# Rotary embedding on one core: tiles of 8 positions held in place from load to store, with the first and last tile in pieces and the tables on the load queue

## The chip, the cores and the metric

The kernel runs on one core of one Trainium2 chip. The metric is device time in microseconds (us), the median of several executions. All runs told of here were in the fast state, with a granted clock of 1.00 in every profile. A profile's span is some 1.5 to 2.3 us shorter than the median time.

## The reference

`x` is float32 of shape (8, 2048, 16, 64), 67.11 MB; `cos` and `sin` are (2048, 32), 262 KB each. Each pair of neighbouring elements of a head is rotated by the angle of its position:

```python
x1, x2 = x_pairs[..., 0], x_pairs[..., 1]
out1 = x1 * cos - x2 * sin
out2 = x1 * sin + x2 * cos
out = np.stack([out1, out2], axis=-1)      # float32, the shape of x
```

So 134.74 MB must pass between HBM, the chip's main memory, and the core, whatever the kernel does; the profile counts 134.76 MB, with 0.02 MB of instructions.

## The kernel before

A tile is 128 partitions with 4 positions each: 4096 float32 per partition, 16 KB, 2.1 MB in all. There are 32 tiles. For each, the sync engine's queue loads it; ScalarE (ACT) rounds it to bfloat16 ("halve"); VectorE (DVE) makes two products with tables and one sum ("rotate"); ACT widens the result into an output buffer and issues the store from its own queue.

```python
K = 4; NX = 5                       # positions per partition; x buffers
# pools: xt x 5 (16 KB), xh qt pt x 2 (8 KB each), ot x 4 (16 KB)

def load(i):    nc.sync.dma_start(out=xt, in_=x_t[b, g])
def halve(i):   nc.scalar.copy(out=xh, in_=xt)                  # to bf16
def rotate(i):  # qt = xh * sin_table ; pt = xh * cos_table ; pt += swap(qt)
    ...
def store(i):
    nc.scalar.copy(out=ot, in_=pt)                              # to f32
    nc.scalar.dma_start(out=out_t[b, g], in_=ot)

load(0)
nc.scalar.dma_start(out=cos_sb, in_=cos_t)      # both on ACT's queue
nc.scalar.dma_start(out=sin_sb, in_=sin_t)
for i in range(1, NX): load(i)
# ... DVE builds s_tab and c_tab from sin_sb and cos_sb ...
halve(0)
for i in range(n):
    if i + 1 < n: halve(i + 1)
    rotate(i); store(i)
    if i + NX < n: load(i + NX)
```

Order matters on ACT, which runs its list in order: a store that has to wait holds back every halving behind it. The library that places the waits has eight completion semaphores for DMAs and gives them out in turn, so each DMA must also wait until the one eight places before it has landed (read from the instruction list of the built kernel).

## Time and profile before

| | before |
|---|---|
| time, median | 329.98 us (329.9 to 330.17) |
| span of the profile | 328.5 us |
| DVE busy, ACT busy | 218.3 us (66%), 230.8 us (70%) |
| moved, mean rate | 134.76 MB, 410 GB/s |
| sine table landed | 34.6 us |
| first store issued | 46.4 us |

Three views matter. The slices give, for each fortieth of the span, the busy share of an engine in tenths and the rate of the DMAs. The busy time by stretches gives the same for stretches that one chooses. The waits say who waited for whom. The prediction below shows lines of each. The timeline, in order of start, shows what the wait does (start us, duration us, engine, line, operation, and in brackets the idle time before it with its releaser; ACTq and SPq are the queues from which ACT and the sync engine issue DMAs):

```profile
34.63 0.45 DVE L102 CAST s_tab<-sin_sb 128x512 bf16<-128x512 f32 x1 [34.63 <-DMA sin_sb<-in_sin_dram]
42.75 3.61 ACT L91 CAST ot<-pt 128x4096 f32<-128x4096 bf16 x1 [25.37 <-DVE pt L85]
46.39 0.37 ACTq L92 DMA_DIRECT2D out_dram<-ot  x1
```

The sine table's cast starts the moment the table has landed; ACT had stood 25.37 us with two tiles halved when it widened the first result; the first store follows. Until then the output direction of the DMAs had nothing to do.

### The profile page before, as it was taken

How to read it: one execution, taken by the hardware profiler on the slowest of the kernel's cores; microseconds unless marked ns; L12 is line 12 of the kernel's file. 1: busy time of each engine (PE TensorE's matmuls, PEld its weight loads, DVE VectorE, ACT ScalarE, POOL GpSimd, SP SyncE). 2: the span in 40 equal slices, each digit the busy share in tenths (PEclk: the TensorE clock that was granted, in tenths of full speed). 3: DMA queues.
4: the chain of work that ended last, by engine and by line, in shares of the span. 5: the costliest groups of instructions: out<-in, count | busy, mean ns of one | idle time of the engine just before them, and what ended most of it. 6: DMA issues, size and time to landing. Idle time of an engine off the chain costs nothing.

```text
span 328.5 us, 334 instructions
## 1 busy us (share of the span) xinstructions
DVE 218.3 (66%) x99; ACT 230.8 (70%) x65; POOL 0.2 (0%) x4
## 2 busy tenths in 40 slices
DVE  0000798899999999866668866667876666876910
ACT  1710079999999999676786676687677678669740
POOL 0000000000000000000000000000000000000000
DMA  7999739999999999999999999999999999999997
GB/s 295 427 423 425 268 140 353 405 427 435 427 435 429 437 425 437 424 435 427 436 427 435 427 435 429 433 429 433 429 433 429 433 429 433 429 435 427 435 427 315
DMA packets 10275, 134.76 MB, mean 410 GB/s; under 512 B 1057, under 2 KB 2081, under 8 KB 2081
## 3 DMA queue, kind: packets, MB, share of 16 engines
q1 hardware_dynamic: 4608, 67.11, 48.7%
q10 hardware_dynamic: 5664, 67.64, 48.4%
q14 instruction: 3, 0.02, 0.0%
HBM read 67.63 MB, written 67.11 MB: 410 GB/s over the span
## 4 chain that ended last, share of the span: by engine, by line
DMA 62%; ACT 24%; issue 5%; DVE 4%; ACTq 1%
DMA out_dram<-ot 52%; ACT ot L91 18%; DMA sin_sb<-in_sin_dram 10%; ACT xh L60 6%; DVE pt L85 1%; DVE qt L79 1%; DVE pt L80 1%; ACTq L92 1%; ACTq L96 0%; DVE s_tab L102 0%; DVE s_tab L103 0%; ACTq L91 0%; DVE c_tab L104 0%
## 5 line engine op out<-in xcount | busy, mean ns | idle before, releaser
L91 ACT CAST ot<-pt 128x4096 f32<-128x4096 bf16 x32 | 115.3, 3604 | 64.7 <-DMA out_dram<-ot 36.0
L60 ACT CAST xh<-xt 128x4096 bf16<-128x4096 f32 x32 | 115.4, 3605 | 19.5 <-ACT ot L91 12.4
L79 DVE TENSOR_TENSOR qt<-xh,s_tab 128x4096 bf16<-128x4096 bf16 x32 | 73.3, 2291 | 59.2 <-ACT xh L60 59.2
L85 DVE TENSOR_TENSOR pt<-pt,qt 128x4096 bf16<-128x4096 bf16 x32 | 73.3, 2292 | 1.1
L80 DVE TENSOR_TENSOR pt<-xh,c_tab 128x4096 bf16<-128x4096 bf16 x32 | 73.1, 2284 | 0.0
L102 DVE CAST s_tab<-sin_sb 128x512 bf16<-128x512 f32 x1 | 0.5, 454 | 34.6 <-DMA sin_sb<-in_sin_dram 34.6
L60 ACT ACT_TABLE_LOAD x1 | 1.3, 1283 | 1.8 <-issue 1.8
L104 DVE CAST c_tab<-cos_sb 128x1024 bf16<-128x1024 f32 x1 | 0.7, 684 | 0.0
L103 DVE TENSOR_SCALAR s_tab<-sin_sb 128x512 bf16<-128x512 f32 x1 | 0.4, 442 | 0.0
L130 POOL MEMSET const-bfloat16-1.0<- 128x1 bf16 x1 | 0.1, 102 | 0.0
L130 POOL MEMSET const-uint8-127<- 128x1 uint8 x1 | 0.1, 102 | 0.0
L130 POOL MEMSET const-float32-0.0<- 128x1 f32 x1 | 0.1, 99 | 0.2 <-issue 0.2
L130 POOL MEMSET const-float32-1.0<- 128x1 f32 x1 | 0.1, 99 | 0.0
## 6 DMA issues: line engine op xcount, KB each, us to landing
xt<-in_x_dram SPq DMA_DIRECT2D x32, 2048.0 KB, 31.0
out_dram<-ot ACTq DMA_DIRECT2D x32, 2048.0 KB, 32.0
cos_sb<-in_cos_dram ACTq DMA_DIRECT2D x1, 256.0 KB, 22.7
sin_sb<-in_sin_dram ACTq DMA_DIRECT2D x1, 256.0 KB, 33.4
```

Source lines behind the costliest of these rows:

```text
L60: nc.scalar.copy(out=xh, in_=loaded.pop(i))
L79: nc.vector.tensor_tensor(out=rows(qt), in0=rows(xh), in1=tab(s_tab), op=mult)
L80: nc.vector.tensor_tensor(out=rows(pt), in0=rows(xh), in1=tab(c_tab), op=mult)
L85: nc.vector.tensor_tensor(out=pt3, in0=pt3, in1=q_swap, op=add)
L91: nc.scalar.copy(out=ot, in_=rotated.pop(i))
L92: nc.scalar.dma_start(out=out_t[b, g], in_=ot)
L102: nc.vector.tensor_copy(out=s2[:, :, 0], in_=sin_flat)
L103: nc.vector.tensor_scalar_mul(s2[:, :, 1], sin_flat, -1.0)
L104: nc.vector.tensor_copy(out=c_tab.rearrange("p g k (i j) -> p (g k i) j", j=2), in_=cos_sb.rearrange("p g c -> p (g c)").to_broadcast([P, ...
L130: nc = _bacc.Bacc("TRN2", target_bir_lowering=False, num_devices=1)
```

## The change

The intent: larger packets and fewer DMAs (tiles of 8 positions, 32 KB per partition), no output buffers (the result goes back over x, so one buffer serves from load to store), a quick start (first tile in pieces, tables behind it on the load queue) and a short end (last tile in pieces). The buffers take 200 KiB per partition before and after. The diff is shortened: `...` marks what is left out, and the pool lines and the comments stand for longer code.

```diff
-    K = 4
+    K = 8
-    hpool: xh, qt, pt x 2;  opool: ot x 4
+    hpool: xh x 3, qt x 1;  no opool
+    first_runs = [(0, 1), (1, 2), (2, 4), (4, 8)]
+    last_runs  = [(0, 4), (4, 6), (6, 7), (7, 8)]
+    # load_runs / store_runs: whole tile, but first_runs for the load of
+    # tile 0 and last_runs for the load and the store of the last tile
+    # computing: two halves per tile; tiles 0 and n-1 by those runs
...
-        nc.vector.tensor_tensor(out=rows(pt), in0=rows(xh), in1=tab(c_tab), op=mult)
+        nc.vector.tensor_tensor(out=rows(xh), in0=rows(xh), in1=tab(c_tab), op=mult)
...
-        ot = opool.tile([P, W], fp32, name="ot")
-        nc.scalar.copy(out=ot, in_=rotated.pop(i))
-        nc.scalar.dma_start(out=out_t[b, g], in_=ot)
+        nc.scalar.copy(out=tiles[i][:, k0:k1], in_=rotated.pop(j)[:, : k1 - k0])
+        for r0, r1 in store_runs(i):
+            if r1 == k1:
+                nc.scalar.dma_start(out=out_t[b, g, :, r0:r1], in_=tiles[i][:, r0:r1])
+        if k1 == K and i + NX < n:
+            load(i + NX)
...
-        nc.scalar.dma_start(out=cos_sb, in_=cos_t)
-        nc.scalar.dma_start(out=sin_sb, in_=sin_t)
+        nc.sync.dma_start(out=cos_sb, in_=cos_t)
+        nc.sync.dma_start(out=sin_sb, in_=sin_t)
```

More of the change, by code (lines that the diff above doesn't have):

```diff
@@ L26 @@
     P = 128
-    K = 4
+    K = 8
     G = S // (P * K)
     D2 = D // 2
-    W = K * H * D
+    HD = H * D
     NX = 5
-    x_t = x.rearrange("b (g p k) h d -> b g p (k h d)", p=P, k=K)
-    out_t = out.rearrange("b (g p k) h d -> b g p (k h d)", p=P, k=K)
+    x_t = x.rearrange("b (g p k) h d -> b g p k (h d)", p=P, k=K)
+    out_t = out.rearrange("b (g p k) h d -> b g p k (h d)", p=P, k=K)
     cos_t = cos.rearrange("(g p k) c -> p g (k c)", p=P, k=K)
@@ L39 @@
     xpool = ctx.enter_context(tc.tile_pool(name="xpool", bufs=NX))
-    hpool = ctx.enter_context(tc.tile_pool(name="hpool", bufs=2))
-    opool = ctx.enter_context(tc.tile_pool(name="opool", bufs=4))
+    hpool = ctx.enter_context(tc.tile_pool(name="hpool", bufs=1))
     cos_sb = consts.tile([P, G, K * D2], fp32)
@@ L49, with load_runs, store_runs, halve @@
     n = len(groups)
-    loaded, halved, rotated = {}, {}, {}
+    first_runs = [(0, 1), (1, 2), (2, 4), (4, 8)]
+    last_runs = [(0, 4), (4, 6), (6, 7), (7, 8)]
+    def load_runs(i):
+        return first_runs if i == 0 else last_runs if i == n - 1 else [(0, K)]
+    def store_runs(i):
+        return last_runs if i == n - 1 else [(0, K)]
+    pieces = []
+    for i in range(n):
+        runs = first_runs if i == 0 else last_runs if i == n - 1 else [(0, 4), (4, 8)]
+        pieces += [(i, k0, k1) for k0, k1 in runs]
+    tiles, halved, rotated = {}, {}, {}
     def load(i):
         g, b = groups[i]
-        xt = xpool.tile([P, W], fp32, name="xt")
-        nc.sync.dma_start(out=xt, in_=x_t[b, g])
-        loaded[i] = xt
-    def halve(i):
-        xh = hpool.tile([P, W], bf16, name="xh")
-        nc.scalar.copy(out=xh, in_=loaded.pop(i))
-        halved[i] = xh
-    def rotate(i):
+        tiles[i] = xpool.tile([P, K, HD], fp32, name="xt")
+        for k0, k1 in load_runs(i):
+            nc.sync.dma_start(out=tiles[i][:, k0:k1], in_=x_t[b, g, :, k0:k1])
+    def halve(j):
+        i, k0, k1 = pieces[j]
+        halved[j] = hpool.tile([P, 4, HD], bf16, name="xh", bufs=3)
+        nc.scalar.copy(out=halved[j][:, : k1 - k0], in_=tiles[i][:, k0:k1])
+    def rotate(j):
+        i, k0, k1 = pieces[j]
         g, _ = groups[i]
-        xh = halved.pop(i)
-        qt = hpool.tile([P, W], bf16, name="qt")
-        pt = hpool.tile([P, W], bf16, name="pt")
+        nk = k1 - k0
+        xh = halved.pop(j)
+        qt = hpool.tile([P, 4, HD], bf16, name="qt")
         def rows(a):
-            return a.rearrange("p (k h e) -> p k h e", k=K, h=H, e=D)
+            return a[:, :nk].rearrange("p k (h e) -> p k h e", h=H, e=D)
         def tab(a):
@@ L74, in tab, with widen @@
                 a,
-                offset=a.offset + g * K * D,
-                ap=[a.ap[0], [D, K], [0, H], [1, D]],
+                offset=a.offset + (g * K + k0) * D,
+                ap=[a.ap[0], [D, nk], [0, H], [1, D]],
             )
         nc.vector.tensor_tensor(out=rows(qt), in0=rows(xh), in1=tab(s_tab), op=mult)
-        nc.vector.tensor_tensor(out=rows(pt), in0=rows(xh), in1=tab(c_tab), op=mult)
+        nc.vector.tensor_tensor(out=rows(xh), in0=rows(xh), in1=tab(c_tab), op=mult)
         q_swap = dataclasses.replace(
-            qt, offset=qt.offset + 1, ap=[qt.ap[0], [2, W // 2], [-1, 2]]
+            qt, offset=qt.offset + 1, ap=[qt.ap[0], [2, nk * HD // 2], [-1, 2]]
         )
-        pt3 = pt.rearrange("p (a j) -> p a j", j=2)
-        nc.vector.tensor_tensor(out=pt3, in0=pt3, in1=q_swap, op=add)
-        rotated[i] = pt
-    def store(i):
-        g, b = groups[i]
-        ot = opool.tile([P, W], fp32, name="ot")
-        nc.scalar.copy(out=ot, in_=rotated.pop(i))
-        nc.scalar.dma_start(out=out_t[b, g], in_=ot)
+        xh3 = xh[:, :nk].rearrange("p k (a j) -> p (k a) j", j=2)
+        nc.vector.tensor_tensor(out=xh3, in0=xh3, in1=q_swap, op=add)
+        rotated[j] = xh
+    def widen(j):
+        i, k0, k1 = pieces[j]
+        nc.scalar.copy(out=tiles[i][:, k0:k1], in_=rotated.pop(j)[:, : k1 - k0])
+        g, b = groups[i]
+        for r0, r1 in store_runs(i):
[3 more added lines that the diff above has]
+            load(i + NX)
     with tc.manual_schedule():
         load(0)
-        nc.scalar.dma_start(out=cos_sb, in_=cos_t)
-        nc.scalar.dma_start(out=sin_sb, in_=sin_t)
+        nc.sync.dma_start(out=cos_sb, in_=cos_t)
+        nc.sync.dma_start(out=sin_sb, in_=sin_t)
         for i in range(1, NX):
@@ L108 @@
         halve(0)
-        for i in range(n):
-            if i + 1 < n:
-                halve(i + 1)
-            rotate(i)
-            store(i)
-            if i + NX < n:
-                load(i + NX)
+        for j in range(len(pieces)):
+            if j + 1 < len(pieces):
+                halve(j + 1)
+            rotate(j)
+            widen(j)
 _INS = ['x', 'cos', 'sin']
```

## The prediction

> **What bounds the kernel now.** I began with the page: is any compute engine full, and if not, what is? VectorE (DVE) is busy 66% of the span and ScalarE (ACT) 70%; the DMA row is at 9 in nearly every slice, except in three places. The first fence is the slice view: one character per fortieth of the span (8.2 us), then the rate moved in each slice.
>
> ```profile
> DVE  0000798899999999866668866667876666876910
> ACT  1710079999999999676786676687677678669740
> ...
> DMA  7999739999999999999999999999999999999997
> GB/s 295 427 423 425 268 140 353 405 427 435 427 435 429 437 425 437 424 435 427 436 427 435 427 435 429 433 429 433 429 433 429 433 429 433 429 435 427 435 427 315
> ```
>
> The reader is to see that the rate is 424 to 437 from the ninth slice to the last but one, and that the holes are slice 1, slices 5 to 8 and slice 40. To size the holes I asked for the busy time by stretches, cut where the rate changes (columns: stretch, length, DVE, ACT, POOL busy, clock, DMA share, GB/s):
>
> ```profile
> 0.00:4.00 4.00, 0.00 (x0) 1.28 (x1) 0.20 (x4) 1.00 0.57 165
> 4.00:32.00 28.00, 0.00 (x0) 7.21 (x2) 0.00 (x0) 1.00 1.01 422
> 32.00:48.00 16.00, 13.30 (x9) 4.81 (x2) 0.00 (x0) 1.00 0.53 202
> 48.00:62.00 14.00, 12.25 (x6) 13.15 (x5) 0.00 (x0) 1.00 0.98 366
> 62.00:324.00 262.00, 192.74 (x86) 204.38 (x57) 0.00 (x0) 1.00 1.01 431
> 324.00:328.50 4.50, 0.00 (x0) 0.00 (x0) 0.00 (x0) 1.00 0.49 211
> ```
>
> For 262 of 328.5 us the kernel moves 431 GB/s with the DMA engines full. The page gives 134.76 MB in all; at 431 GB/s that is 312.7 us. The rest of the span is lost DMA time, and each stretch's loss is its length times (1 - rate/431): 2.5 us at the start, 0.6 us from 4 to 32, **8.5 us** from 32 to 48, **2.1 us** from 48 to 62, 2.3 us at the end: 16.0, and 312.7 + 16.0 = 328.7, the span. So the ledger closes, and only the holes can be won.
>
> Why the middle hole? The waits, first of the engines, then of the loads' queue (SPq), say it:
>
> ```profile
> DVE s_tab L102 <- DMA sin_sb<-in_sin_dram: 34.6, 1, 34.6
> ACT ot L91 <- DVE pt L85: 28.7, 2, 25.4
> ...
> SPq L55 <- DMA cos_sb<-in_cos_dram: 20.1, 1, 20.1
> SPq L55 <- DMA sin_sb<-in_sin_dram: 10.8, 1, 10.8
> ```
>
> No rotation can start before the sine table is there, at 34.6 us, although it is 256 KB. ACT has halved two tiles by then and stands, the first store goes out at 46.4 us (timeline), and the five x buffers are not freed. The load queue itself waits for both tables: the instruction list of the kernel before shows eight completion semaphores taken in turn by all DMAs, so each DMA waits for the one eight places earlier; loads 5 and 6 come eight after the two tables. From 42 to 46 us the rate is 0.
>
> **What the Trainium skill says.** (1) "DMA: Bandwidth & Descriptors", section "Queues, rings and completion order": each DMA engine takes turns between queues that have work, a packet at a time. The trace agrees: the tables are 1,024 packets of 512 B on ACT's queue, 64 on each of 16 engines. At 431/16 = 26.9 GB/s a 16 KB packet of x takes 0.61 us; if each table packet waits for one of x, 64 take 39 us, 32 (cosine) 19.5. They landed 33.4 and 22.7 us after issue, and x had nothing to send for part of that time. (2) Same page, "Where 436 GB/s comes from": the fabric's ceiling is 435.2 GB/s. The trace sustains 431, so larger packets can win at most 1%, 3 us; I expect nearly none. (3) "SBUF — State Buffer", "SBUF size: 192, 224, or 256?": about 208 KiB per partition are usable. The sums below stay at 200; the trace cannot show it. (4) "VectorE: DVE Perf Modes", the section on the TRN2 errata: ScalarE needs 224 cycles plus one per element at 1.2 GHz. For 4096 elements 3.60 us; the trace has 3.605.
>
> **The change, part by part.** *Tables* move to the load queue, behind x's first tile, in front of the second. They no longer alternate with x packets. First tile plus tables are 4.19 + 0.52 = 4.72 MB; at 422 GB/s from 2.5 us on they end at 13.7; with an estimated 1 us to landing, 15 us. Against 34.6 that is **20 us earlier**, in compute. Table preparation costs 1.3 us as before (34.63 to 35.91 in the timeline).
>
> *First store.* Tile 0 is cut 1+1+2+4 of 8 positions. From the durations of 4096 elements (ACT 3.605, DVE 2.29), pieces of 1024 and 2048 cost by the formula of (4) 1.04 and 1.89 us on ACT; for DVE I estimate 0.69 and 1.22 (1.07 us saved per halving, as two bf16 per cycle at 0.96 GHz give). ACT works in order, halving one piece ahead: three operations per piece put the rotations at 16.3-18.4, 18.4-20.5, 21.3-25.0 and 25.9-32.8; ACT then halves the first half of tile 1, until 31.4, and widens from 32.8 to 36.4. The first store goes out at about **37 us** instead of 46.4, of 4.19 MB. Meanwhile five tiles are loading: 20.97 + 0.52 MB need 51 us at 422 GB/s, to 53 us. So stores join 16 us before the first loads are used up, and the engines **never run dry**. The losses of 8.5 and 2.1 us go away.
>
> *In-place result.* The output buffers go, and a tile is held from load to store: 5 x 32 KB, three xh and one qt of 8 KB, tables 8 KB, 200 KiB; before it was 5 x 16 + 4 x 16 + 6 x 8 + 8 = 200. The price is that a load waits for the landing of a store. In steady state a tile's load and store need 8.39 MB / 431 = 19.5 us, its compute the larger of ACT 4 x 3.605 + issues (15.1, twice the 7.52 between successive stores where the trace runs ACT-bound, 61.48 to 69.01) and DVE 6 x 2.29 = 13.7. Compute has 4.4 us of slack per tile. It holds up to two tiles, because a tile's last widening stands behind the halving of the next tile. Three remain with the DMAs; one would do to keep them full. Eight semaphores make each DMA wait for the one about four tiles back: loose enough.
>
> *Tail.* By my count the last load lands near 281 us; ACT gets through its last pieces near 298, while stores of three tiles remain, to 315. So the DMAs stay the bound to the end, then the last store needs its landing: the 2.3 us of before.
>
> *Compute totals.* ACT: 14 tiles x 14.42 + 2 x 15.15 = 232 us (before 231); DVE: 14 x 13.74 + 2 x 14.67 + 1.6 = 223 (before 218). All beside the DMAs.
>
> *Sum.* 312.7 + start 2.5 + about 0.6 for the loads-only rate + 0.3 for 1 and 4 KB packets (my estimate) + end 2.3 = 318.4 us of span. The medians lie 1.5 us above the span (329.98 against 328.5): **319.7 us**, 3.2% faster.
>
> **The rivals.** *Too few buffers.* Load waits for store, a round trip of 2 x 19.5 us plus compute; if compute held four of five tiles, the DMAs would thin out in mid-span. For it: the same 200 KiB are now freed in lumps of 32 KB. Against it: compute's slack. If it cost 0.5 us per tile, 16 tiles would make it 328. *Tracking by whole tile.* If the widening of the last tile's second piece waited for the store of its first (same buffer, other region), the final four pieces would go one by one behind landings, some 3 to 5 us each: about 328. The trace has no such case, so I cannot exclude it; I give it 7%. *The hidden gain.* Were the early hole only covering a later compute limit, nothing would come. Against it: from 62 to 324 us ACT works 204 of 262 us. *Faster packets.* At the ceiling of 435 the sum falls by 2.9 us, to 317.
>
> **Range and chances.** Most uncertainty is downward in gain: 316.5 to 324. Faster by over 2% needs less than 323.5 us: 0.86. Within 2%: 0.12, the rivals. Slower by over 2%: 0.02.
>
> **What would show it.** The sine table lands near 15 us and DVE starts near 16; the first store is issued near 37; the slices show no hole between the second and the last; the middle runs at 430 to 433; waits of the loads for stores are long on their queue but the DMA share stays at 1.0; at the end ACT is done some 15 us before the span. It is wrong if mid-span slices fall below 425, if the last stores stand apart from each other, or if a hole remains between 30 and 60 us.

## The result, and the profile after

The changed kernel takes **318.62 us** (318.48 to 319.15, 4 runs) against 330.0 of the kernel before on the same chip: a ratio of 0.9658, 95% interval 0.9641 to 0.9674. A ratio is the mean time of one kernel's fast runs over that of the other's of the same rounds, so not quite the ratio of the medians. The forecast was 319.7 us in a range of 316.5 to 324.0, so it held.

The slices of the kernel after:

```profile
DVE  0189999999999596693967939588440999999112
ACT  4078899999998692976949679495803999997322
...
DMA  7999999999999999999999999999999999999997
GB/s 304 424 463 405 455 397 401 459 438 422 455 405 463 397 460 401 459 414 448 443 418 455 405 459 405 455 405 459 418 443 447 414 428 430 424 433 439 442 414 302
```

The holes of slices 5 to 8 are gone: the DMA row is at 9 from the second slice to the last but one. By stretches:

```profile
0.00:4.00 4.00, 0.00 (x0) 1.28 (x1) 0.20 (x4) 1.00 0.53 168
4.00:32.00 28.00, 15.76 (x15) 14.69 (x8) 0.00 (x0) 1.00 1.03 437
32.00:48.00 16.00, 14.93 (x8) 15.20 (x5) 0.00 (x0) 1.00 0.98 406
48.00:62.00 14.00, 13.06 (x7) 13.54 (x5) 0.00 (x0) 1.00 1.04 449
62.00:312.00 250.00, 179.45 (x84) 184.89 (x56) 0.00 (x0) 1.00 1.00 432
312.00:316.90 4.90, 0.00 (x0) 0.40 (x1) 0.00 (x0) 1.00 0.57 232
```

The rate in single slices swings between 397 and 463, while the kernel before, with packets of 16 KB, had 424 to 437. I put that down to packets being booked as a whole (the DMA share of a stretch can pass 1.00, as the 1.04 above), so sums over longer stretches are what to read. Against the 431 GB/s of the ledger in the prediction the losses are 2.4 us at the start, 0 from 4 to 62 us (437, 406 and 449 offset each other), a gain of 0.6 from 62 to 312, and 2.3 at the end: 312.7 + 4.1 = 316.8, the span of 316.9. The waits of the engines, then of the load queue:

```profile
ACT xh L75 <- DMA xt<-in_x_dram: 61.6, 13, 12.7
DVE s_tab L121 <- DMA sin_sb<-in_sin_dram: 14.4, 1, 14.4
SPq L70 <- DMA out_dram<-xt: 241.9, 11, 51.4
```

The sine table is there at 14.4 us in place of 34.6. The load queue now stands 241.9 us for stores, as it must when a buffer is free only after its store, and the engines of the DMAs never run out of work over it: the longest total wait of the trace costs nothing. The two ends of the timeline, first store and last tile:

```profile
35.94 0.37 ACTq L109 DMA_DIRECT2D out_dram<-xt  x1
...
288.08 1.90 ACT L75 CAST xh<-xt 128x2048 bf16<-128x2048 f32 x1 [1.92 <-DMA xt<-in_x_dram]
299.00 1.04 ACT L75 CAST xh<-xt 128x1024 bf16<-128x1024 f32 x1 [5.52 <-DMA xt<-in_x_dram]
308.10 1.04 ACT L75 CAST xh<-xt 128x1024 bf16<-128x1024 f32 x1 [6.25 <-DMA xt<-in_x_dram]
312.43 0.34 ACTq L109 DMA_DIRECT2D out_dram<-xt  x1
```

The first store goes out at 35.9 us (46.4 before). The last tile's second, third and fourth piece land at 288.1, 299.0 and 308.1 us, and ACT, which waits for each (1.9, 5.5 and 6.3 us), issues the last store at 312.4, only 4.5 us before the end. That is not what the prediction had.

### The profile page after: what moved, and what is told of

The parts are those of the page before. It is cut to its first block, busy times and chain, and to the rows that moved or that the text cites. A ratio compares the mean times of both kernels' runs of the same rounds, so it can differ in the third digit from the quotient of the medians.

```text
span 316.9 us, 352 instructions
## 1 busy us (share of the span) xinstructions
DVE 223.2 (70%) x111; ACT 230.0 (73%) x73; POOL 0.2 (0%) x4
## 4 chain that ended last, share of the span: by engine, by line
DMA 62%; ACT 26%; DVE 4%; issue 3%; another core or an unknown queue 2%; SPq 1%; ACTq 1%
DMA xt<-in_x_dram 31%; DMA out_dram<-xt 28%; ACT xt L105 14%; ACT xh L75 12%; DMA sin_sb<-in_sin_dram 4%; DVE xh L100 1%; DVE xh L95 1%; DVE qt L94 1%; SPq L70 1%; ACTq L109 1%; DVE s_tab L121 0%; SPq L115 0%; DVE s_tab L122 0%; ACTq L105 0%
## 5 line engine op out<-in xcount | busy, mean ns | idle before, releaser
L75 ACT CAST xh<-xt 128x4096 bf16<-128x4096 f32 (+2 forms) x36 | 116.1, 3224 | 66.9 <-DMA xt<-in_x_dram 61.6
L105 ACT CAST xt<-xh 128x4096 f32<-128x4096 bf16 (+2 forms) x36 | 116.0, 3223 | 14.8 <-DVE xh L100 14.4
L94 DVE TENSOR_TENSOR qt<-xh,s_tab 128x4096 bf16<-128x4096 bf16 (+2 forms) x36 | 74.0, 2055 | 71.2 <-ACT xh L75 70.3
L100 DVE TENSOR_TENSOR xh<-xh,qt 128x4096 bf16<-128x4096 bf16 (+2 forms) x36 | 74.0, 2055 | 1.2
L95 DVE TENSOR_TENSOR xh<-xh,c_tab 128x4096 bf16<-128x4096 bf16 (+2 forms) x36 | 74.0, 2055 | 1.2
L121 DVE CAST s_tab<-sin_sb 128x512 bf16<-128x512 f32 x1 | 0.5, 453 | 14.4 <-DMA sin_sb<-in_sin_dram 14.4
## 6 DMA issues: line engine op xcount, KB each, us to landing
out_dram<-xt ACTq DMA_DIRECT2D x1, 2048.0 KB, 17.6
```

The lines of the kernel that those rows point to most:

```text
L75: nc.scalar.copy(out=halved[j][:, : k1 - k0], in_=tiles[i][:, k0:k1])
L94: nc.vector.tensor_tensor(out=rows(qt), in0=rows(xh), in1=tab(s_tab), op=mult)
L95: nc.vector.tensor_tensor(out=rows(xh), in0=rows(xh), in1=tab(c_tab), op=mult)
L100: nc.vector.tensor_tensor(out=xh3, in0=xh3, in1=q_swap, op=add)
L105: nc.scalar.copy(out=tiles[i][:, k0:k1], in_=rotated.pop(j)[:, : k1 - k0])
L121: nc.vector.tensor_copy(out=s2[:, :, 0], in_=sin_flat)
```

## The experiments

Eleven further kernels and the changed one again were run, all correct. "Before" was between 330.16 and 330.27 us on those chips.

| run | one edit | median us | ratio to before (95%) |
|---|---|---|---|
| e1 | before, tables behind the first load | 319.58 | 0.9676 (0.9661 to 0.9690) |
| e2 | before, tables behind the fifth load | 325.72 | 0.9860 (0.9846 to 0.9875) |
| e3 | after, tables on ACT's queue | 319.07 | 0.9659 (0.9643 to 0.9675) |
| e4 | e3, first tile not in pieces | 331.55 | 1.0035 (1.0022 to 1.0048) |
| e5 | after, last load whole | 318.61 | 0.9650 (0.9636 to 0.9663) |
| e6 | after, last store whole | 324.44 | 0.9825 (0.9811 to 0.9838) |
| e7 | after, last tile wholly as the others | 318.45 | 0.9644 (0.9631 to 0.9657) |
| e8 | after, three tiles held in place of five | 366.35 | 1.1113 (1.1082 to 1.1145) |
| e9 | after, tiles of 4, ten held | 329.95 | 0.9993 (0.9985 to 1.0001) |
| e10 | e9, last load whole | 321.46 | 0.9734 (0.9721 to 0.9748) |
| e11 | e10, eight held | 320.03 | 0.9692 (0.9679 to 0.9705) |
| after again | beside e9 | 318.73 | 0.9652 (0.9638 to 0.9665) |

### Which part of the change earns it?

**e1.** The kernel before with two words changed:

```diff
-        nc.scalar.dma_start(out=cos_sb, in_=cos_t)
-        nc.scalar.dma_start(out=sin_sb, in_=sin_t)
+        nc.sync.dma_start(out=cos_sb, in_=cos_t)
+        nc.sync.dma_start(out=sin_sb, in_=sin_t)
```

> The kernel before with one edit: both table loads go to the load queue behind the first x tile; tiles of 4, five x and four output buffers as before. Theory (the gain is the early hole, and the hole is the wait for the tables): sine lands near 10 us, the first store goes out near 22 us, no hole between 32 and 62 us, time 319 to 321 us, nearly all of the 11.4 us gained. Rival (large tiles, 32 KB packets or the in-place buffers earn it): the hole shrinks but the time stays above 325 us.

Measured: 319.58 us. The rate by slices of e1:

```profile
GB/s 273 416 429 431 429 431 429 433 433 433 437 433 431 429 429 429 428 431 431 430 429 433 431 439 431 433 433 429 429 429 429 431 431 429 431 433 433 437 431 316
```

From the waits of e1, the one for the sine table:

```profile
DVE s_tab L102 <- DMA sin_sb<-in_sin_dram: 10.4, 1, 10.4
```

The table is there at 10.4 us, the first store goes out at 22.8, and no hole is left. Of the 3.42% that the whole change saves, this edit alone saves 3.24%. The rival, that large tiles and in-place buffers earn the bulk of it, is out; the 0.18% left over for them is not clear of noise, as the intervals of e1 and of the kernel after overlap.

**e2.** The same two loads, but placed behind the fifth load of x.

> The kernel before with both table loads on the load queue, but behind all five first x loads. A middle dose. Theory: the tables land near 29 us (11.0 MB at 422 GB/s from 2.5 us on, and a little), so the first store goes out near 41 us, 5 us earlier than before and some 19 us later than with the tables behind the first tile; the seven loads that can run before the first store end near 38.5 us, so a hole of some 4.5 us and a slow start remain: 324 to 327 us. Rival (only the mixing of small packets with x packets cost time): as fast as with the tables behind the first tile, 319 to 321.

Measured: 325.72 us, inside the range. The table landed at 29.8 us, the first store went out at 41.56, and the slices show the shortened hole:

```profile
GB/s 294 426 444 393 324 304 361 434 432 430 436 428 432 434 430 432 429 432 428 433 436 428 430 436 428 432 432 432 430 430 438 430 430 436 426 432 430 434 430 324
```

Slices 4 to 7 hold 393, 324, 304 and 361 where before it was 425, 268, 140 and 353. Here the tables do not share turns with anything on another queue, and they still cost 6 us: it is the time at which they land that counts, through the first store, not the mixing as such.

**e3.** The kernel after with the tables back on ACT's queue (the diff of e1 reversed).

> The kernel after with the tables back on ACT's queue. Theory (taking turns packet by packet): 32 table packets per DMA engine now alternate with the 32 small packets of the first tile's four pieces, so the tables land with that tile, near 13 to 15 us, and the time stays within 0.5% of the kernel after, 318 to 320 us. Rival (the other queue as such delays them): they land past 25 us and the time goes past 322.

Measured: 319.07 us, ratio 0.9659 against 0.9658 of the kernel after. The table landed at 12.9 us. So in the changed kernel the queue of the tables does not matter, because the small packets of the first tile's pieces leave them their turns.

**e4.** e3, and the first tile loaded and computed as the others:

```diff
-        return first_runs if i == 0 else last_runs if i == n - 1 else [(0, K)]
+        return last_runs if i == n - 1 else [(0, K)]
-        runs = first_runs if i == 0 else last_runs if i == n - 1 else [(0, 4), (4, 8)]
+        runs = last_runs if i == n - 1 else [(0, 4), (4, 8)]
```

> The kernel after with the tables back on ACT's queue and the first tile loaded and computed as the others (one load of 32 KB packets, two halves). Theory: each of 32 table packets per engine waits for a 32 KB packet of 1.22 us, so sine lands near 40 us, the first store goes out near 60 us, five loads are used up at 53 us and load 5 waits for the first store: holes of 9 to 14 us, time 327 to 335 us, all of the gain lost. Rival (pieces of the first tile and the place of the tables do not matter): 319 us.

Measured: 331.55 us, 0.35% above the kernel before, so all of the gain is lost. The rate by slices of e4:

```profile
GB/s 326 428 426 449 406 445 127 191 381 354 409 445 445 433 433 405 445 441 434 441 417 429 438 441 441 413 425 441 441 441 433 413 433 445 437 433 431 429 405 288
```

From its timeline, the first widening, with ACT's idle time before it, and the first store:

```profile
50.81 3.60 ACT L105 CAST xt<-xh 128x4096 f32<-128x4096 bf16 x1 [30.25 <-DVE xh L100]
...
61.49 0.36 ACTq L109 DMA_DIRECT2D out_dram<-xt  x1
```

Sine lands at 42.5 us (estimated 40), the first store goes out at 61.5 (60), and slices 7 and 8 fall to 127 and 191 GB/s. The two tables have 32 packets per engine; if each waits for a 32 KB packet of x, 1.22 us at 26.9 GB/s, that makes 39 us. This is the 39 us that the prediction has for the kernel before, where 64 packets wait 0.61 us each: with tiles of 8 a wait is twice as long, but the tables have half as many packets, of 1 KB. e3 shows that the pieces of the first tile are a cure. The place in the queue is shown to be one for tiles of 4 (e1); for tiles of 8 without pieces it was not run by itself.

The five points together, in order of the sine table's landing:

| | sine landed | first store | time |
|---|---|---|---|
| e1 | 10.4 | 22.8 | 319.58 |
| after | 14.4 | 35.9 | 318.62 |
| e2 | 29.8 | 41.6 | 325.72 |
| before | 34.6 | 46.4 | 329.98 |
| e4 | 42.5 | 61.5 | 331.55 |

A first store before the first loads are used up costs nothing, however early it is (e1 against after). Beyond that each microsecond of delay costs about one (e2 to before: 4.8 us later and, on the same chip, 4.5 us longer). With tiles of 8 that point lies later, near 53 us by the prediction's count of 20.97 + 0.52 MB at 422 GB/s; with tiles of 4 only seven loads fit before the first store, 15.2 MB or 38.5 us. Counted from these two estimated points, e2, before and e4 are 3.1, 7.9 and 8.5 us late and lost 6.1, 10.7 and 12.5 us (against e1, e1 and e3): some 3 to 4 us are lost on top, whatever the delay. In the kernel before, the slow restart from 48 to 62 us is 2.1 of them; the rest was not traced.

### The last tile

**e5, e6, e7.** Why did the last load land at 308 us, not at 281? My theory was that the two queues take turns packet by packet, so a load of small packets beside stores of 32 KB packets gets a small share. The edits, in the two functions that cut the last tile:

```diff
 def load_runs(i):
-    return first_runs if i == 0 else last_runs if i == n - 1 else [(0, K)]
+    return first_runs if i == 0 else [(0, K)]            # e5, e7
 def store_runs(i):
-    return last_runs if i == n - 1 else [(0, K)]
+    return [(0, K)]                                      # e6, e7
 # e7 computes the last tile in two halves too
```

> The kernel after, with the last tile loaded whole (32 KB packets) while its computing and its stores stay in four pieces. Theory (queues take turns packet by packet, so a load of 16, 8 and 4 KB packets gets 1/3, 1/5 and 1/9 of the engines beside stores of 32 KB packets): the last load lands near 280 us instead of 308, ACT ends near 298 instead of 312; the time stays within 0.5% of the kernel after (317.5 to 319.5), because the bytes left are the same and the DMAs stay full. Rival (the last load came late because few loads were in flight): it lands past 300 us again.

> The kernel after, with the last tile stored in one piece, its load still in four. Theory: the last small piece of the load lands near 308 us, the store of 4.19 MB can go out only near 312 us, when the other stores are done, and needs 9.7 us alone plus its landing: 325 to 328 us, some 7 us lost. Rival (a backlog of stores covers it, as the prediction had it with ACT done at 298): 318 to 320 us.

> The kernel after, with the last tile treated as any other: loaded whole, computed in two halves, stored whole. Theory: the load lands near 280 us, its store goes out near 300 us while earlier stores still run, so the time stays within 0.6% of the kernel after (317.5 to 320.5): the pieces of the last tile only pay for the delay that they cause. Rival (stores in pieces at the end are needed as such): 324 us or more.

Measured: e5 318.61 us, e6 324.44 (0.6 below its range, but far from its rival's 318 to 320), e7 318.45. In the timeline of e5 the halving of the last tile starts when its load has landed, and the last store follows:

```profile
280.70 3.60 ACT L75 CAST xh<-xt 128x4096 bf16<-128x4096 f32 x1 [4.73 <-DMA xt<-in_x_dram]
...
302.92 0.34 ACTq L109 DMA_DIRECT2D out_dram<-xt  x1
```

The whole load of 4.19 MB lands at 280.7 us; cut in pieces to be early, its last piece landed at 308.1. So the rival of e5, too few loads in flight, is out. ACT's last store went out at 302.9, where 298 was expected. The size fits the theory: a piece of 0.524 MB in 4 KB packets beside 32 KB packets gets 4 of 36 bytes, and 0.524 x 9 / 431 GB/s is 10.9 us; the third piece took 299.0 - 288.1 = 10.9, the fourth 9.1. In e6 the late pieces meet a store that cannot go out before them; it was issued at 310.84 us. The rate by slices of e6:

```profile
GB/s 309 435 426 455 390 435 410 455 439 406 455 439 406 452 439 406 455 439 407 451 439 410 451 439 410 451 439 410 451 439 410 451 424 422 428 434 440 329 195 325
```

Slices 38 and 39 fall to 329 and 195 GB/s. With the load whole, e7 stores whole as well and loses nothing, because its store goes out at 302.6 us behind stores that still run. So the pieces of the last load cost 27 us of lead, and the pieces of the last store only pay for that. The net is zero: after, e5 and e7 have ratios of 0.9658, 0.9650 and 0.9644 whose intervals overlap. e7 is the best of the study by its median, but not clearly ahead of the changed kernel (which gave 0.9652 when run again); it is the simpler one.

### How many tiles must be held

**e8.** `NX = 5` becomes `NX = 3`.

> The kernel after with three tiles in place of five. The prediction had three of five with the DMAs where one would do. Theory: a tile of three is away for load and store at most 27 us of each 58 us cycle, less than the 2 x 19.5 us that a shared load and store take, so in turns only one queue has work and there are gaps behind each landing: 322 to 345 us, with mid-span slices below 425 GB/s. Rival (one in flight is enough): 318 to 320 us.

Measured: 366.35 us, 15% above the kernel after and beyond the range I gave. Its slices:

```profile
DMA  8995989799897997989989899898998979979998
GB/s 324 424 453 237 457 291 403 309 396 446 288 403 302 388 454 237 417 331 404 403 284 410 342 374 428 291 403 345 378 428 288 446 302 403 432 230 433 434 429 345
```

The rate swings between full and 230 to 300. ACT waits 107.3 us for loads (61.6 with five). A store must wait until the next tile has landed, because ACT halves one piece of the next tile first; with three tiles, load and store of the others then run side by side for 19 us (both land 19 us after issue, by the median) and are through almost together. In one round the load lands at 111.9 us and ACT works 7 us on it, so the next store is issued at 119.0; the next load is issued at 115.6, when the running store has landed; and from 114 to 116 us the rate is 0. Over the run this comes to 48 us, some 3 per tile. One tile in flight on average is not the same as one at every moment. Four tiles were not tried.

### The size of the tile alone

**e9.** The kernel after with tiles of 4, ten held in place, so the same bytes:

```diff
-    K = 8
+    K = 4
-    NX = 5
+    NX = 10
-    first_runs = [(0, 1), (1, 2), (2, 4), (4, 8)]
-    last_runs = [(0, 4), (4, 6), (6, 7), (7, 8)]
+    first_runs = [(0, 1), (1, 2), (2, 4)]
+    last_runs = [(0, 2), (2, 3), (3, 4)]
```

with one piece per other tile.

> The kernel after with tiles of 4 positions (16 KB packets), ten of them held, first and last tile in three pieces: the same bytes held, half the tile. It measures tile size alone. Theory (packet size earns at most the step from 431 to about 433 GB/s in mid-span): 318.5 to 320.5 us, within 0.5% of the kernel after. Rival (32 KB packets are a gain of their own): over 321 us, mid-span at 431 GB/s or less. A third way: eight semaphores in turn hold back loads of small tiles and leave gaps.

> The changed kernel itself, on the same chip in the same rounds as the run with tiles of 4, to compare the two: 318.6 us as before, within 0.3%.

Measured: 329.95 us, against 318.73 for the changed kernel in the same rounds. All of the gain was gone, which I had not expected. By its letter the rival holds (over 321 us, mid-span at 431 GB/s or less), but not in its reason: the mid-span runs at 431 as in the kernel before and in e1, which kept the gain. The loss is at the end. The end of e9 by stretches:

```profile
240.00:262.00 22.00, 4.88 (x3) 1.48 (x1) 0.00 (x0) 1.00 1.01 430
262.00:285.00 23.00, 15.95 (x7) 20.05 (x6) 0.00 (x0) 1.00 1.01 431
285.00:295.00 10.00, 9.29 (x6) 9.18 (x4) 0.00 (x0) 1.00 0.73 311
295.00:310.00 15.00, 13.73 (x6) 14.18 (x5) 0.00 (x0) 1.00 0.66 280
```

And ACT's timeline there, with the idle time in brackets:

```profile
234.37 3.60 ACT L75 CAST xh<-xt 128x4096 bf16<-128x4096 f32 x1 [12.31 <-DMA out_dram<-xt]
263.75 0.34 ACTq L109 DMA_DIRECT2D out_dram<-xt  x1
264.13 3.60 ACT L75 CAST xh<-xt 128x4096 bf16<-128x4096 f32 x1 [22.64 <-DMA xt<-in_x_dram]
271.65 3.60 ACT L75 CAST xh<-xt 128x4096 bf16<-128x4096 f32 x1 [0.41 <-ACT xt L105]
```

From 240 to 262 us the DMAs are full and ACT does 1.48 us of work; from 262 on ACT works almost without a break, 7.52 us per tile, and from 285 on the rate falls to 311 and 280: ACT's own pace. It had fallen behind while it stood 12.31 us before one store and 22.64 before the next, both with a result ready. The instruction list says what for: the DMA eight places back. (The third way had named these semaphores, but as a brake on the loads; here they hold back stores.) With three load pieces at the end, the two stores wait for the landing of a store one later than usual, and of the load of tile 29.

**e10, e11.** Two ways to loosen that wait: load the last tile whole, so that two DMAs fewer stand between (e10); and, on top of that, hold only eight tiles (`NX = 8`), so that loads run less far ahead (e11).

> The kernel in place with tiles of 4 and ten of them held, which came out at 330 us, with one edit: its last tile is loaded whole, so two load DMAs fewer. The trace of the run at 330 shows full DMAs until 285 us, ACT standing 12 and 22 us before stores it had ready, then 60 us of ACT at its own pace. Theory (a store is issued by ACT in order and must wait for the DMA eight places before it, because eight completion semaphores are taken in turn; the three pieces of the last load move the ninth store from the end from a wait for the load of tile 28 to one for tile 29, which runs slowly beside larger packets): the long stop shrinks to some 10 us or less, time 319 to 325 us. Rival (tiles of 16 KB packets lose in themselves): 329 to 331 again.

> The same, with eight tiles of 4 held in place of ten (16 MB in place of 20). Theory of the semaphores: the loads run only eight tiles ahead, so the load for which a late store waits is three tiles ahead of it instead of five and has landed by then; no long stop of ACT, 318.5 to 321 us, as fast as the kernel after with four fifths of its buffers. Rival (fewer buffers are worse): slower than with ten, 325 us or more.

Measured: e10 321.46 us, e11 320.03, both in their ranges, so tiles of 16 KB packets do not lose in themselves. Not all of the theory held. In e10 the stop of 12 us was gone and the long one was not: 23.7 us, where I had 10 or less. The store after the long stop went out at 255.13 us in place of 263.75, 8.6 us earlier, and the time fell by 8.5. In e11 a stop of 12.8 us was left, where I had none; the slices show that it cost nothing:

```profile
GB/s 266 414 428 430 430 428 430 435 435 435 430 430 428 430 433 429 427 430 430 435 435 433 428 428 430 433 430 430 430 428 435 437 433 430 428 428 433 433 430 311
```

Fewer buffers were faster here, since less work was left undone when the loads were through.

Why the long stop in e10 stayed as long can be read from its chain that ended last (start us, us, what):

```profile
188.10 36.11 DMA out_dram<-xt
...
224.26 30.80 DMA xt<-in_x_dram
...
255.13 0.34 ACTq L109
```

The store at 255.13 us must wait for the DMA eight places before it, the load of tile 28. That load was itself issued only at 224.26 us, when a store had landed. The last store before the stop went out at the same moment (224.28), and the load then took 30.8 us. ACT had 7 us of work in that time and stood for the other 23.7. e9 has the same with the load of tile 29: issued at 233.95, it took 29.7 us. So the edit moved the stop one load forward and did not shorten it.

Between e11 and the changed kernel 1.3 us remain. The first 4 us moved 119 GB/s in e11 and 168 after, 0.5 us at the full rate; from 4 to 62 us it is 428 against 431 GB/s, 0.4 us, and from 62 to 312 us 431 against 432, 0.6 us. So larger packets can have earned some 1 us of rate at most. Sums as small as these are near what the booking of whole packets blurs: 0.52 MB, one 32 KB packet on each of 16 engines, is 1.2 us at 431 GB/s.

## Why the prediction was right

- **The ledger and the hole: right.** What there was to win were the 10.6 us of the middle hole, and the change won 11.4. e1 and e2 show its cause, the late tables, and the size per microsecond. Steps on the way: tables at 15 us (14.4), DVE from 16 (15.7 with the first product), first store near 37 (35.9), pieces of 1024 and 2048 elements on DVE at 0.69 and 1.22 us (0.69 and 1.23), ACT 232 us (230.0), DVE 223 (223.2).
- **The sum: 1.5 us too high.** It said 318.4 us of span, and it was 316.9. The terms that were mis-sized are the loads-only rate, set at a loss of 0.6 us, and the small pieces at 0.3: measured from 4 to 62 us the loss was 0. A further 0.6 us came from 432 GB/s in place of 431. Its last step is a slip: 318.4 and the 1.5 us from span to median make 319.9, not 319.7, and 319.7 would be 3.1% less time than 329.98, not 3.2%.
- **Larger packets: right.** "Nearly none" was expected; e11 bounds it at some 1 us of rate.
- **The in-place step: right in its result, wrong in its reason.** "Three remain with the DMAs; one would do to keep them full" fails: with two tiles fewer the time is 366 us. Compute's slack of 4.4 us per tile was true and did not help, since it is not a rate that is missing but a load or store at the moment when both queues run empty. That five tiles were enough was therefore partly luck; how many are needed between three and five is not known.
- **The tail: wrong in size, without a price.** "The last load lands near 281 us; ACT gets through its last pieces near 298." It was 308.1 and 312.4. The step that failed let loads and stores share evenly to the end. I had used the turns packet by packet for the tables, and not for the small pieces of the last load. For a whole load, e5, 281 was right to half a microsecond (280.7), and 298 was 302.9. The 15 us of reserve were 4.5, and e6 shows that with the load in pieces and the store whole 5.8 us of the gain would have gone. That the time held is partly luck: by the prediction's count a whole last store would have cost nothing, and only because it was cut all the same did the late load do no harm.
- **The eight semaphores: "loose enough" held for tiles of 8 as run, and not for ten tiles of 4.** e9 lost all of the gain while ACT stood before its stores, and e10 won most of it back with one edit to the last load. No rival that I had named covers this; the order of a few DMAs at the end decided 8.5 us.
- **Tracking by whole tile: out.** The second piece of the last tile was widened at 299.95 us, while the store of its first piece, issued at 293.5 and 17.6 us on its way, was still running.

## What to carry to other kernels

When the DMAs are full in mid-span, add up what each stretch loses against that rate, and look for what holds the first store: here two small tables, behind which nothing could be computed, cost nearly as much as the whole rework won, and two words cure it. A small transfer beside a queue of large packets is served by count, not by bytes: put it on the same queue in the right place, and do not cut a last load into small packets while large stores run. When results go out in place, test the number of buffers and the order of the last DMAs by themselves, since an engine that works in order may stand before a store that waits for a load.

## What the Trainium skill lacked or had wrong

- "DMA: Bandwidth & Descriptors", section "Issuing engines are not separate DMA queues": it says that DMAs from different engines interleave on the same 16 DMA engines, and that issuing from several only saves sequencer time. Which queue the tables were on changed the time from 330.27 to 319.58 us (e1) with no other edit. It fits that a queue of 512 B packets has to wait for one of 16 KB at each turn; in e3, beside the small packets of the first tile's pieces, the queue made no difference (ratio 0.9659 against 0.9658).
- The turns by packet that the prediction quotes from the same page are what the runs show; the page does not draw the consequence that a queue's share goes with its packet size. Measured: 0.524 MB in 4 KB packets took 10.9 us beside 32 KB packets, and a last load landed at 308.1 us in pieces, at 280.7 whole.
- The same page, section "Where 436 GB/s comes from", says that for transfers between HBM and SBUF the HBM side at about 358 GB/s binds. One core alone sustained 431 to 432 GB/s, reads and writes together, over 250 us. Other pages of the skill already give a core that runs alone more than 358.
- No page that I read has the wait of a DMA for the one eight places before it. It is the library's doing, not the chip's; in e9 it held ACT for 12.31 and 22.64 us before stores that were ready.
